# A first weight tile loaded in five uneven parts instead of two even ones, in a DMA-bound sliding-window matmul

One NeuronCore of a Trainium2 chip runs the kernel. The metric is the device time of one launch in microseconds (us). The kernel before takes 182.14 us, median of six runs (181.95 to 182.30).

## The reference

```python
B, S, D, W = 4, 4096, 4096, 64      # x [B,S,D] fp32, w [D,D] fp32
for b in range(B):
    o = int(offsets[b])
    results.append(x[b, o:o+W] @ w)  # four windows of 64 rows, all times the same w
```

All of `w` (67 MB) has to be read once for 256 rows of output.

## The kernel before

The weights are read k tile by k tile (128 rows each) and multiplied in fp16 on the matrix engine (PE). All tiles but the first come over GpSimd's software DMA queue, which converts fp32 to fp16 on the way. The first tile comes as fp32 over the sync queue (SP) and is cast by ScalarE, so that the DMA engines have work before the software queue's first packet, at 5.46 us. A packet is one piece that a DMA engine moves, here a part of one row.

```python
w0_32 = acc[1]                                             # scratch until the sums start
nc.sync.dma_start(out=w0_32[:, :NG], in_=w[0:P, :NG])      # 128 x 2048 fp32, 1 MB
nc.scalar.dma_start(out=off_t[:], in_=offsets[None, :])
nc.sync.dma_start(out=w0_32[:, NG:], in_=w[0:P, NG:])      # the other 1 MB
nc.scalar.copy(out=w_one[0][:, :NG], in_=w0_32[:, :NG])
nc.scalar.copy(out=w_one[0][:, NG:], in_=w0_32[:, NG:])
...
nc.gpsimd.dma_start(out=w_one[1][:], in_=w[P : 2 * P, :])  # software queue: tile 1, x, then the rest
...
q = [nc.scalar, nc.sync]                                   # the last four stores
store(q[g], g, c0, c0 + NG // 2)
```

## Time and profile before

| | before |
|---|---|
| time, median | 182.14 us |
| span in the profile | 180.1 us |
| PE busy | 71% |
| DMA queues, share of 16 engines | 99.7% |
| first weight data; last landing | 1.88; 179.24 us |

The lines of the page, of the windows and of the timeline stand in the prediction below. One more view: the chain of work that ended last, in order of time (start, length, what). Its two long waits for weights before were these:

```profile
6.85 36.17 DMA wc<-in_w_dram
...
78.30 42.09 DMA wc<-in_w_dram
```

The first wide load (4 MB) that the chain waits for is complete at 6.85 + 36.17 = 43.02 us.

Beside these views I use the records of the trace behind them: the start and length of every DMA packet, and the sixteen completion times of every load, one for each DMA engine. A load tells that it has landed by a semaphore, a counter that it raises. "Late" below means behind the median of the sixteen.

### The profile page before, as it was taken

The page shows a single profiled execution, that of the slowest core. Times are in us where ns is not written, and L with a number is a line of the kernel's source. Part 1 is how long each engine was busy: PE and PEld are TensorE (multiplying, and loading weights), DVE is VectorE, ACT ScalarE, POOL GpSimd, SP SyncE. Part 2 cuts the span into 40 slices and gives each one's busy share as a digit, 9 for nine tenths or more (in the row PEclk, how much of TensorE's full clock was granted, in tenths as well). Part 3 has the DMA queues.
Part 4 walks back from the last instruction along what each step waited for, and adds up shares of the span by engine and source line. Part 5 has one row for each costly group of instructions (what it writes and reads, how often), then busy time and mean ns, then how long its engine had stood idle before and what let it go on. Part 6 is the DMA issues. An engine that isn't in the chain of part 4 may idle for free.

```text
span 180.1 us, 1403 instructions
## 1 busy us (share of the span) xinstructions
PE 128.2 (71%) x576; PEld 57.3 (32%) x576; DVE 82.2 (46%) x68; ACT 16.9 (9%) x15; POOL 12.7 (7%) x27
## 2 busy tenths in 40 slices
PE   0000789104999499938996599949999999999910
PEld 0000764001344134413442134414444444443400
DVE  0000566200276427642566036733778975407560
ACT  2422346200000000000000000000000004004000
POOL 4600000000000100010001000020007100000200
PEclk9999999855599969996999569987999999999995
DMA  5999979999998899999989999999999999999996
GB/s 187 313 260 213 286 160 211 236 233 226 233 233 175 182 233 233 236 218 233 204 175 218 233 233 220 222 193 202 229 206 215 198 211 213 214 214 207 338 412 241
DMA packets 4151, 40.97 MB, mean 227 GB/s; under 512 B 434, under 2 KB 434, under 8 KB 2226
## 3 DMA queue, kind: packets, MB, share of 16 engines
q0 software_dynamic: 3280, 36.70, 93.5%
q1 hardware_dynamic: 576, 3.15, 4.6%
q10 hardware_dynamic: 290, 1.05, 1.5%
q8 instruction: 4, 0.07, 0.1%
q14 instruction: 1, 0.01, 0.0%
HBM read 71.30 MB, written 4.19 MB: 419 GB/s over the span
## 4 chain that ended last, share of the span: by engine, by line
DMA 43%; PE 43%; issue 4%; DVE 2%; another core or an unknown queue 1%; POOLq 1%; DVEq 1%; POOL 1%
DMA wc<-in_w_dram 43%; PE banks L154 43%; DVE acc L164 2%; DVEq L263 1%; POOLq L75 1%; POOL xrow L82 0%; POOL identity masks.py:197 0%; POOLq L82 0%; POOL w L71 0%; POOLq masks.py:199 0%; DVEq L164 0%; POOLq L252 0%
## 5 line engine op out<-in xcount | busy, mean ns | idle before, releaser
L154 PE MATMUL banks<-wc,xT 128*128 128x512 f16 x480 | 115.8, 405 | 23.6 <-DMA wc<-in_w_dram 23.3
L164 DVE TENSOR_TENSOR acc<-acc,banks 128x1024 f32<-128x1024 f32 x56 | 67.9, 1221 | 69.0 <-PE banks L154 68.4
L154 PEld LDWEIGHTS <-xT 128*128 128x128 f16 x512 | 52.3, 103 | 93.9 <-DMA wc<-in_w_dram 26.4
L140 PE MATMUL banks<-identity,xrow 128*128 128x128 f16 x64 | 5.3, 261 | 19.9 <-DMA xrow<-in_x_dram 19.9
L209 ACT COPY tmp<-banks 128x1024 f32<-128x1024 f32 x4 | 3.9, 1016 | 128.2 <-PE banks L154 128.2
L149 DVE CAST xT<-banks 128x1024 f16<-128x1024 f32 x4 | 4.8, 1222 | 21.5 <-PE banks L140 21.5
L99 POOL DMA_DIRECT2D wc<-in_w_dram x8 | 4.3, 539 | 108.1 <-PE banks L154 108.1
L140 PEld LDWEIGHTS <-xrow 128*128 128x128 f16 x64 | 5.1, 127 | 20.0 <-issue 20.0
L154 PE MATMUL banks<-w,xT 128*128 128x512 f16 x32 | 7.1, 379 | 0.0
L182 DVE COPY acc<-banks 128x1024 f32<-128x1024 f32 x4 | 4.9, 1225 | 1.6 <-PE banks L154 1.6
L118 POOL DMA_DIRECT2D wc<-in_w_dram x6 | 3.9, 674 | 17.1 <-PE banks L154 17.1
L213 DVE TENSOR_TENSOR acc<-acc,tmp 128x1024 f32<-128x1024 f32 x4 | 4.7, 1218 | 0.0
L151 ACT CAST xT<-banks 128x1024 f16<-128x1024 f32 x4 | 4.0, 1014 | 7.9 <-PE banks L140 7.9
L184 ACT COPY acc<-banks 128x1024 f32<-128x1024 f32 x4 | 4.0, 1012 | 3.0 <-PE banks L154 3.0
L200 POOL DMA_DIRECT2D out_dram<-acc x2 | 1.1, 537 | 27.2 <-DVE acc L213 27.2
L68 ACT CAST w<-acc 128x2048 f16<-128x2048 f32 x1 | 1.9, 1898 | 4.8 <-DMA acc<-in_w_dram 4.8
L82 POOL DMA_DIRECT2D xrow<-in_x_dram x4 | 2.1, 524 | 2.1 <-issue 2.1
L67 ACT CAST w<-acc 128x2048 f16<-128x2048 f32 x1 | 1.9, 1898 | 3.1 <-DMA acc<-in_w_dram 3.1
L67 ACT ACT_TABLE_LOAD x1 | 1.3, 1283 | 1.4 <-PEq L252 1.4
L71 POOL DMA_DIRECT2D w<-in_w_dram x1 | 0.7, 660 | 0.8 <-POOLq L252 0.8
masks.py:199 POOL TENSOR_SCALAR_AFFINE_SELECT identity<-identity 128x128 f16<-128x128 f16 x1 | 0.3, 287 | 0.1
masks.py:197 POOL MEMSET identity<- 128x128 f16 x1 | 0.2, 223 | 0.0
(4 smaller groups left out, 0.4 us busy)
## 6 DMA issues: line engine op xcount, KB each, us to landing
wc<-in_w_dram POOLq DMA_DIRECT2D x5, 4096.0 KB, 42.1
wc<-in_w_dram POOLq DMA_DIRECT2D x4, 1024.0 KB, 24.5
wc<-in_w_dram POOLq DMA_DIRECT2D x1, 3072.0 KB, 37.1
acc<-in_w_dram SPq DMA_DIRECT2D x2, 1024.0 KB, 8.1
xrow<-in_x_dram POOLq DMA_DIRECT2D x4, 512.0 KB, 14.4
wc<-in_w_dram POOLq DMA_DIRECT2D x1, 2048.0 KB, 26.4
out_dram<-acc POOLq DMA_DIRECT2D x2, 1024.0 KB, 5.6
w<-in_w_dram POOLq DMA_DIRECT2D x1, 1024.0 KB, 11.8
```

Of the source, the lines that this page charges most:

```text
L67: nc.scalar.copy(out=w_one[0][:, :NG], in_=w0_32[:, :NG])
L99: nc.gpsimd.dma_start(out=t[:, base : base + r * N], in_=w[k0 * P : (k0 + r) * P, :].rearrange("(p r) n -> p (r n)", r=r),)
L118: nc.gpsimd.dma_start(out=t[:, pos : pos + n * wd].rearrange("p (t n) -> p t n", t=n), in_=w[ki * P : (ki + n) * P, ng * NG + c0 : ng * NG ...
L140: nc.tensor.matmul(out=pairs[t][:, i * P : (i + 1) * P], lhsT=x_cols(g, 8 * t + i), rhs=identity[:], start=True, stop=True,)
L149: nc.vector.tensor_copy(out=dst, in_=pairs[t][:])
L151: nc.scalar.copy(out=dst, in_=pairs[t][:])
L154: nc.tensor.matmul(out=banks(bank), lhsT=xT[g][:, kt * P : (kt + 1) * P], rhs=rhs, start=start, stop=stop,)
L164: nc.vector.tensor_add(out=dst, in0=dst, in1=banks(bank, n))
L182: nc.vector.tensor_copy(out=dst, in_=banks(b0, 2))
L184: nc.scalar.copy(out=dst, in_=banks(b0, 2))
L209: nc.scalar.copy(out=tmp[g][:], in_=banks(4 * g + 2, 2))
L213: nc.vector.tensor_add(out=dst, in0=dst, in1=tmp[g][:])
```

## The change

The intent, as I read it: a load of 12 rows uses twelve DMA engines and one of 4 rows four of them, so the parts 12, 4 and 112 take a row of 4 KB from four engines and give one more to four others. As the first DMAs of the queue the small parts should, by this intent, cost nothing.

```diff
     w0_32 = acc[1]
-    nc.sync.dma_start(out=w0_32[:, :NG], in_=w[0:P, :NG])
+    Q = N // 4
+    for r0, r1, c0, c1 in (
+        (0, 12, 3 * Q, N),
+        (12, 16, 3 * Q, N),
+        (0, P, 0, NG),
+        (16, P, 3 * Q, N),
+        (0, P, NG, 3 * Q),
+    ):
+        nc.sync.dma_start(out=w0_32[r0:r1, c0:c1], in_=w[r0:r1, c0:c1])
     nc.scalar.dma_start(out=off_t[:], in_=offsets[None, :])
-    nc.sync.dma_start(out=w0_32[:, NG:], in_=w[0:P, NG:])
```

## The prediction

> **What bounds the kernel now.** I began with the page: the rows of 40 slices, the queues and the HBM total.
>
> ```profile
> PE   0000789104999499938996599949999999999910
> DMA  5999979999998899999989999999999999999996
> q0 software_dynamic: 3280, 36.70, 93.5%
> q1 hardware_dynamic: 576, 3.15, 4.6%
> q10 hardware_dynamic: 290, 1.05, 1.5%
> q8 instruction: 4, 0.07, 0.1%
> HBM read 71.30 MB, written 4.19 MB: 419 GB/s over the span
> ```
>
> PE has low slices. DMA has one low slice at each edge and is at eight tenths or more elsewhere, apart from one 7. Its queues add up to 99.7% of the sixteen engines' span. So I asked the view of windows where DMA work starts and ends. The last two columns are DMA share and GB/s.
>
> ```profile
> 1.00:1.50 0.50, 0.00 (x0) 0.00 (x0) 0.00 (x0) 0.08 (x1) 0.11 (x1) 1.00 0.00 0
> 1.50:2.00 0.50, 0.00 (x0) 0.00 (x0) 0.00 (x0) 0.50 (x1) 0.50 (x1) 1.00 0.64 131
> 2.00:2.50 0.50, 0.00 (x0) 0.00 (x0) 0.00 (x0) 0.50 (x1) 0.42 (x3) 1.00 0.98 147
> 3.50:4.00 0.50, 0.00 (x0) 0.00 (x0) 0.00 (x0) 0.00 (x0) 0.46 (x1) 1.00 1.00 426
> ...
> 177.50:178.00 0.50, 0.00 (x0) 0.00 (x0) 0.00 (x0) 0.00 (x0) 0.00 (x0) 0.50 1.02 410
> 178.00:178.50 0.50, 0.00 (x0) 0.00 (x0) 0.00 (x0) 0.00 (x0) 0.00 (x0) 0.50 0.54 213
> 178.50:179.00 0.50, 0.00 (x0) 0.00 (x0) 0.00 (x0) 0.00 (x0) 0.00 (x0) 0.50 0.06 25
> ```
>
> (In these lines the figure before the DMA share is the granted clock.) Data moves from about 1.9 to about 178.4 us with hardly a gap, and the stores at the end go straight on after the loads. 71.30 + 4.19 = 75.49 MB in 176.5 us is 428 GB/s, or 26.7 GB/s for each of 16 engines. The kernel is bound by DMA end to end. Only three things can move its end: idle time of the DMA engines, packet overhead, and an uneven share between them. The chain of waits puts 43% on PE, because PE still has queued work after a late load, but the loads and stores behind it have no gap either.
>
> The timeline of the first microseconds shows the part that changes:
>
> ```profile
> 0.87 0.38 SPq L64 DMA_DIRECT2D acc<-in_w_dram  x1
> 1.30 0.42 SPq L66 DMA_DIRECT2D acc<-in_w_dram  x1
> 5.80 1.90 ACT L67 CAST w<-acc 128x2048 f16<-128x2048 f32 x1 [3.10 <-DMA acc<-in_w_dram]
> 12.53 1.90 ACT L68 CAST w<-acc 128x2048 f16<-128x2048 f32 x1 [4.83 <-DMA acc<-in_w_dram]
> 18.31 3.40 PE L140 MATMUL banks<-identity,xrow 128*128 128x128 f16 x32 [18.31 <-DMA xrow<-in_x_dram]
> 25.21 7.07 PE L154 MATMUL banks<-w,xT 128*128 128x512 f16 x32
> ```
>
> SP issues one DMA per 0.43 us (0.87 to 1.30). The first data packet starts at 1.88 us in the packet records, 1.01 us after its issue. The casts of the first k tile end at 14.43, and PE uses them only at 25.21, so 10.8 us are spare: when this tile lands is not on the path. What matters is what its transfer does to the engines.
>
> **Uneven engines.** Every load leaves sixteen completion times, one for each DMA engine. In the last weight load eleven engines finish from 167.7 to 168.3 us and the other five at 168.62, 168.82, 169.01, 169.09 and 169.33. The records also hold five fetches of instructions after the start (four of 16 KB, about 0.9 us each, and one of 8 KB, 0.32 us) at 31.9, 75.5, 111.7, 116.2 and 151.3 us. After each of them one more engine is late in all later loads. So five engines carry something extra, and the latest sets each landing.
>
> **What the Trainium skill says.** "DMA: Bandwidth & Descriptors", section "Why a DMA increments its semaphore by 16 and not by 1", says that a DMA is cut over the largest k up to 16 that divides its slowest dimension, and that from the SP and ACT queues the lowest k engines are used. Twelve rows would then go to engines 0 to 11 and four rows to 0 to 3, one row each, and 112 rows to all, seven each. The trace does not name engines; the [1, 4] load of the offsets leaves one completion packet where a load of 128 rows leaves sixteen, which agrees on k. The same page, "Queues, rings and completion order", says that each engine alternates between its queues; the two queues' packets interleave from 5.5 to 12.5 us here. Thirdly, "Runtime: NRT & Kernel Launch", section "Instruction fetch mechanics", gives 16 KiB blocks, which are the four packets seen; which DMA engines carry them no page that I read says.
>
> **The change, part by part.** The order of instructions differs on SP alone: five loads in place of two, none with a wait. Bytes are unchanged.
> (a) Moved share: engines 0 to 3 get 17 quarter rows of the second half, 4 to 11 get 16 and 12 to 15 get 15. A quarter row is 4096 B; at 26.7 GB/s that is 0.153 us. The intent must be that engines 12 to 15 are the ones with the 16 KB fetches. If so they gain 0.15 us, while 0 to 3 lose 0.15 us out of more than 0.5 us of room. If the late engines are others, this gains nothing or loses 0.15 us.
> (b) Packets: 4096 B packets on the hardware queues took 0.159 us, 8192 B packets 0.309 us. Sixteen of the first less eight of the second: 2.544 - 2.472 = +0.07 us for every engine. Two or three more completion packets of 0.009 to 0.022 us add about 0.03 us. Sum +0.1 us.
> (c) Late start: the first large load is now third on SP. With 0.43 us an issue it begins 2 x 0.43 = 0.86 us later, at about 2.74. In that gap engines move no, one or two quarter rows (0, 0.15, 0.31 us of work). Counted with (a), every engine has the same 15 quarter rows left behind the gap, so all lose 0.86 - 0.15 = 0.71 us against before, with (b) 0.8 us. This is idle time at the front of a saturated stream, and nothing later gives it back.
> (d) Against (c): the start is slow already. Eight packets at 0.309 us from 1.88 would end at 4.35, but the first load's completions come from 4.84 to 5.43, mean 5.13; counted from each engine's own first packet some 0.6 us is lost. First packets took 0.37 to 1.1 us in place of 0.31, while 131 and 147 GB/s moved. If that is a cold start which the small loads now pay inside the gap, up to 0.6 us comes back; if each load after an idle gap pays it anew, none does.
> I take two thirds of (d), 0.4 us: 0.71 + 0.1 - 0.4 = +0.4 us. A shorter distance from issue to data for the second and third loads than the 1.01 us of the first would take off up to another 0.4; half of that leaves +0.2 us.
>
> **Rivals.** First, the rebalancing works as meant: the start's idle time is hidden by the cold start and the late engines save a row, giving -0.15 us or a little more, 182.0. For it: 12, 4 and 112 are exactly the numbers that take a row from engines 12 to 15. Against: SP's issue rate. Second, the full delay: nothing of the cold start is absorbed, +0.8 us, 182.95. For it: no DMA slack anywhere. Third, a PE effect: after a wait PE ran at half the clock (427 ns a matmul against 216 from 120.5 to 123.8); a load landing late against the clock's steps could lengthen a slow stage, at most one step of 3.4 us, 1.7 us of work. Stores now wait for DMA rather than for PE (the last store's add ends at 174.2, its data start at 176.9, about 1.7 us of slack after 1.0 us of issue), which hides most of this: under +0.7 us. Fourth, a later first tile stalls the casts: excluded by the 10.8 us.
>
> **Range and chances.** Runs before lay within 0.16 us. The cases span 182.0 to 183.0, so I predict 182.35 us, with 181.85 to 182.95 for 8 in 10. Two per cent is 3.6 us, which no case reaches.
>
> **What would show it.** SP should issue at about 0.87, 1.30, 1.73, 2.16 and 2.59. If (c) holds, the DMA share between 2.0 and 3.0 us falls well below 0.88, the mean of before's two windows, and the sixteen landings of all later loads shift late together. If the first rival holds, the late engines' landings come 0.15 us earlier and those of four on-time engines later. The prediction is wrong if the casts or PE's last stage set the end, or if the late engines are among 0 to 3, which would add 0.15 us.

## The result, and the profile after

The changed kernel takes 183.76 us, median of six (183.69 to 184.54), against 182.14: 1.62 us more. The ratio is 1.0101, interval 1.0081 to 1.0121; ratios here are the mean time of one kernel's fast runs over that of the other's in the same rounds, so not quite the ratio of the medians. It is a loss clear of noise, and 0.8 us above the top of my range (182.95).

Four rows of the page of after:

```profile
PE   0000769302999499947997499949999999999900
DMA  5999999999799999998999999988999899999995
q1 hardware_dynamic: 736, 3.15, 4.8%
HBM read 71.30 MB, written 4.19 MB: 416 GB/s over the span
```

The bytes are the same, the hardware queue has 736 packets in place of 576, and the rate fell from 419 to 416 GB/s. DMA still bounds the kernel end to end. The windows at both edges (the last two columns are DMA share and GB/s; a packet counts where it starts), first two of before that the prediction doesn't show, then those of after:

```profile
2.50:3.00 0.50, 0.00 (x0) 0.00 (x0) 0.00 (x0) 0.20 (x1) 0.13 (x1) 1.00 0.78 262
3.00:3.50 0.50, 0.00 (x0) 0.00 (x0) 0.00 (x0) 0.00 (x0) 0.00 (x0) 1.00 0.81 311
```

```profile
2.00:2.50 0.50, 0.00 (x0) 0.00 (x0) 0.00 (x0) 0.50 (x1) 0.42 (x3) 1.00 0.13 33
2.50:3.00 0.50, 0.00 (x0) 0.00 (x0) 0.00 (x0) 0.20 (x1) 0.13 (x1) 1.00 1.57 262
3.00:3.50 0.50, 0.00 (x0) 0.00 (x0) 0.00 (x0) 0.00 (x0) 0.00 (x0) 1.00 0.32 115
...
178.50:179.00 0.50, 0.00 (x0) 0.00 (x0) 0.00 (x0) 0.00 (x0) 0.00 (x0) 0.50 1.04 418
179.00:179.50 0.50, 0.00 (x0) 0.00 (x0) 0.00 (x0) 0.00 (x0) 0.00 (x0) 0.50 0.94 377
```

From 2.0 to 2.5 us only 33 GB/s move where 147 moved before. Then sixteen first packets start together (share 1.57) and are slow (115 GB/s in the next half microsecond, where before had 311). The stores run about one microsecond longer. The timeline of after:

```profile
0.87 2.09 SPq L72 DMA_DIRECT2D acc<-in_w_dram  x5
10.10 1.90 ACT L74 CAST w<-acc 128x2048 f16<-128x2048 f32 x1 [7.40 <-DMA acc<-in_w_dram]
21.86 1.90 ACT L75 CAST w<-acc 128x2048 f16<-128x2048 f32 x1 [9.86 <-DMA acc<-in_w_dram]
26.27 7.07 PE L161 MATMUL banks<-w,xT 128*128 128x512 f16 x32
```

SP issued five loads in 2.09 us, 0.42 each, as foreseen. The second half of the tile was complete only at 21.76 us in place of 12.51: each 4 KB packet waited its turn behind a packet of the software queue (0.64 us on average), so fifteen of them per engine lasted longer than eight of 8 KB. The cast and the first multiplication moved by 9.3 and 1.1 us. The chain of after has the same two waits:

```profile
6.84 37.56 DMA wc<-in_w_dram
...
79.61 42.08 DMA wc<-in_w_dram
```

The first wide load is complete at 44.40 in place of 43.02 us, 1.38 later; the second wait is as long as before (42.08 to 42.09). So the transfers lost their time before 44 us, and nothing of it later. The latest engine carries other delays too (an instruction fetch, in the prediction's reading), so for the sums I take the mean of the sixteen completions of this load: 42.05 before, 43.26 after, **+1.21 us**. The last landing of the kernel moved from 179.24 to 180.34, +1.10.

But the span grew by 1.49. The rest is at the very end. Before it is over, SP waits for the semaphore of every DMA in turn. The view of SP's waits, before and after (total us, times, longest):

```profile
SPq L263 <- DMA out_dram<-acc: 4.2, 4, 1.9
```

```profile
SPq L270 <- DMA out_dram<-acc: 4.4, 2, 3.2
```

Before, the four last stores were met one after the other, and the last store's semaphore was last in SP's list: 0.91 us from the last landing (179.24) to the end of the span. After, ten hardware DMAs share eight semaphores, the last store uses that of the first small load again, and this stands early in the list. When it came at 180.36, six more waits of 0.06 us each and what follows them were still to be gone through: 1.29 us from the last landing to the end, **+0.38 us**.

A last part lies outside the profiled span. In the recorded runs the time exceeds the span by 2.00 us on average in after (six runs) and by 1.84 in before (28 runs); of the kernels below on the same chip as before's first rounds, five_big_first has 1.99 and the others 1.82 to 1.87. So the difference of the medians is about the span's 1.49 and this 0.16; what the 0.16 is, no run shows.

### The profile page after: what moved, and what is told of

Read it like the earlier page. It is cut to its first block, busy times and chain, and to the rows that moved or that the text cites. A ratio compares the mean times of both kernels' runs of the same rounds, so it can differ in the third digit from the quotient of the medians.

```text
span 181.6 us, 1414 instructions
## 1 busy us (share of the span) xinstructions
PE 128.1 (71%) x576; PEld 57.3 (32%) x576; DVE 82.2 (45%) x68; ACT 16.6 (9%) x15; POOL 12.7 (7%) x27
## 4 chain that ended last, share of the span: by engine, by line
DMA 44%; PE 42%; issue 4%; DVE 2%; another core or an unknown queue 1%; POOLq 1%; DVEq 1%; POOL 1%
DMA wc<-in_w_dram 44%; PE banks L161 42%; DVE acc L171 2%; DVEq L270 1%; POOLq L82 1%; POOL xrow L89 0%; POOL identity masks.py:197 0%; POOLq L89 0%; POOL w L78 0%; POOLq masks.py:199 0%; DVEq L171 0%; POOLq L259 0%
```

## The experiments

My theory after this reading is a sum: a late start, the 4 KB packets, and the end. The rival is that the uneven share itself made an engine late. Fourteen kernels ran; all gave correct results. Medians are of four runs, all in the fast state (the two marked kernels ran once, state unknown), beside before on the same chip (182.05 to 182.11). `dummy` is a scratch tile that a run adds. The diffs are against before (five_big_first: against after) and are shortened. "Mean" is again the mean completion of the first wide load, 42.05 us in the profile of before.

### 1. The small parts last: five_big_first

```diff
-        (0, 12, 3 * Q, N), (12, 16, 3 * Q, N), (0, P, 0, NG), (16, P, 3 * Q, N), (0, P, NG, 3 * Q),
+        (0, P, 0, NG), (0, P, NG, 3 * Q), (16, P, 3 * Q, N), (0, 12, 3 * Q, N), (12, 16, 3 * Q, N),
```

> The same five loads of the changed kernel on SP, but with the two small ones last. My theory is a sum: the DMA engines idle some 0.75 us while SP issues the two small loads first, the two hardware-generated loads of 4 KB packets and their mixing with the software queue cost 0.1 to 0.5 us, and the waits at the very end cost 0.37 us because ten hardware DMAs share semaphores where before seven did not. This order takes away the idle start alone, so 182.4 to 182.9 us, with the first weight data at 1.9 us as before. Rival: the uneven share (one quarter row more for four engines, one less for four others) is itself the loss; then it stays at 183.6 to 183.9 us.

Measured: 183.39 us, in two pairs, 182.99 and 183.13, 183.66 and 183.68; ratio 1.0076. Mean 42.68, from the last landing to the end 1.29. The late start is gone, and 0.57 of the 1.21 us of mean with it. The median is above what I expected; the lower pair is near, and the upper pair lies where the rival had it. That pair doesn't speak for the rival, though I can't explain it: single runs 0.6 to 0.9 us above the others occur in after (184.4 and 184.5), in two_tiny_first (183.83) and in before itself (182.86 beside 182.05).

### 2. The late start alone: two_tiny_first

```diff
+    for i in range(2):
+        nc.sync.dma_start(out=dummy[0:1, 4*i : 4*i+4], in_=w[0:1, 4*i : 4*i+4])   # 16 bytes each
     nc.sync.dma_start(out=w0_32[:, :NG], in_=w[0:P, :NG])
```

> The kernel before, with two loads of 16 bytes into a scratch tile ahead of the large loads on SP, so the start is late but no share of an engine changes. My theory: the first large load starts 0.8 us later, nothing gives it back, and the end has a semaphore used twice too: 183.1 to 183.5 us. Rival (uneven share): 182.1 to 182.3 us. Rival (a cold start that only has to be paid once, by whoever comes first): 182.3 to 182.7 us.

Measured: 183.00 us, ratio 1.0062, a little under my range. Mean 42.65, +0.60; 1.36 us from the last landing to the end. Its windows at the start:

```profile
2.00:2.50 0.50, 0.00 (x0) 0.00 (x0) 0.00 (x0) 0.50 (x1) 0.42 (x3) 1.00 0.00 0
2.50:3.00 0.50, 0.00 (x0) 0.00 (x0) 0.00 (x0) 0.20 (x1) 0.13 (x1) 1.00 1.40 262
3.00:3.50 0.50, 0.00 (x0) 0.00 (x0) 0.00 (x0) 0.00 (x0) 0.00 (x0) 1.00 0.51 180
```

No data moves for half a microsecond, and the start after it is slow again. Delay alone, without a byte moved to another engine, makes +0.60 us of transfer. The rival of the uneven share foresaw no loss; it can't be the whole. The rival of a cold start that is paid once foresaw 182.3 to 182.7 us. As 0.45 us of the time is the end's, the time alone doesn't exclude it, and the tiny loads are one packet each, so most engines had moved nothing before. The trace of after is the better witness, under (d) below.

### 3. The packets alone: even_split

```diff
-    nc.sync.dma_start(out=w0_32[:, NG:], in_=w[0:P, NG:])
+    nc.sync.dma_start(out=w0_32[:, NG : NG + NG // 2], in_=w[0:P, NG : NG + NG // 2])
+    nc.sync.dma_start(out=w0_32[:, NG + NG // 2 :], in_=w[0:P, NG + NG // 2 :])
```

> The kernel before, with the second half of the first tile loaded as two loads of all 128 rows by 1024 columns: packets of 4 KB, even shares, no late start, eight hardware DMAs in all so that no semaphore is used twice. It prices the packets alone. My theory: 182.2 to 182.6 us, and the first tile's second half lands at 17 to 21 us in place of 12.5, since packets of two queues alternate one for one. Rival (packet size and mixing are the main loss): 183.0 us or more.

Measured: 182.61 us (182.59 to 182.73), ratio 1.0030, with an interval of 0.9999 to 1.0061 since before scattered in these rounds. Mean 42.71, +0.66; the end is as before (0.93 us). The chain shows it:

```profile
6.86 37.00 DMA wc<-in_w_dram
...
79.01 42.14 DMA wc<-in_w_dram
```

The second half's sixteen 4 KB packets took 2.99 us per engine (0.187 each), where eight of 8 KB took 2.57 (0.321 each): +0.42. The software queue's packets beside them took 0.13 more. The first packets started 0.16 later, but the first half's packets then took 0.12 less. The price of a 4 KB packet isn't a fixed one: those of the first of the two loads took 0.202 us, those of the second, which alternated with software packets too, 0.171. At 0.171 sixteen would cost only 0.17 more than before; why the first load was slower isn't shown. Late start and packets, 0.60 + 0.66 = 1.26, meet the 1.21 of the whole change.

### 4. The end alone: three_tiny_last

```diff
     nc.sync.dma_start(out=w0_32[:, NG:], in_=w[0:P, NG:])
+    for i in range(3):
+        nc.sync.dma_start(out=dummy[0:1, 4*i : 4*i+4], in_=w[0:1, 4*i : 4*i+4])
```

> The kernel before, with three loads of 16 bytes on SP behind the large ones: nothing late, nothing moved, ten hardware DMAs in all like the changed kernel. It prices the end alone. My theory: the span from the last landing to the end grows from 0.9 to 1.3 us and the time to 182.4 to 182.6 us. If the end is not charged for semaphores used twice: 182.1 to 182.2 us.

Measured: 182.43 us (182.37 to 182.44); ratio 1.0017 with an interval (0.9986 to 1.0048) that one run of before at 182.86 widens. Mean 42.09, unmoved; the end 1.29 in place of 0.91. SP's waits are those of after in kind, two in place of four, the longest for the last store:

```profile
SPq L266 <- DMA out_dram<-acc: 4.7, 2, 3.4
```

Ten hardware DMAs in place of seven cost the end 0.38 us.

### 5. One more DMA, or smaller packets: rows_split, rows_stride, quarters_woven, first_half_split, one_load

```diff
 # rows_split: second half as rows 0-63 and 64-127; rows_stride: as every other row
+    for r0, r1 in ((0, P // 2), (P // 2, P)):
+        nc.sync.dma_start(out=w0_32[r0:r1, NG:], in_=w[r0:r1, NG:])
+    for r in range(2):
+        nc.sync.dma_start(out=w0_32[r:P:2, NG:], in_=w[r:P:2, NG:])
```

> The second half of the first tile as two loads of 64 rows by 2048 columns: one more DMA than before, as in even_split, but packets stay 8 KB. If the packets of 4 KB cost the 0.56 us that even_split lost, this is at 182.0 to 182.3 us and the first wide load lands at 42.1 us on average, as before; if one more DMA costs it, 182.5 to 182.7 us and 42.7 us.

> The second half as two loads of every other row, 8 KB packets. Against rows_split, whose loads each went to one half of the partitions and lost 1.9 us, each load here is spread over all partitions. If the half of the partitions was what cost there, 182.0 to 182.7 us here, where 182.0 to 182.2 means that one more DMA is free and 182.5 to 182.7 that it is what even_split paid for; if any load of 64 rows costs it, 183.5 us or more.

rows_split took 183.97 us, ratio 1.0098, mean 43.25: a surprise that fits neither theory. Its packets in the second half took 0.36 to 0.64 us on average from one microsecond to the next, in place of 0.32. Each of its loads goes to one half of the partitions only (partitions are the 128 rows of a tile). rows_stride, with as many DMAs and rows in each but spread over all partitions, took 182.25 us, ratio 1.0015, mean 42.09, with packets of 0.32. The first wide wait in the chain, first rows_split, then rows_stride:

```profile
6.84 37.39 DMA wc<-in_w_dram
6.87 36.12 DMA wc<-in_w_dram
```

So one more DMA with 8 KB packets is nearly free, and loads to one block of 64 partitions are not; why their packets are slower isn't shown.

```diff
 # quarters_woven: two loads, each of two separate quarters of the columns (4 KB pieces everywhere)
+    halves = lambda a: a.rearrange("p (h t n) -> p h t n", h=2, t=2)
+    nc.sync.dma_start(out=halves(w0_32[:])[:, :, 0, :], in_=halves(w[0:P, :])[:, :, 0, :])
+    nc.sync.dma_start(out=halves(w0_32[:])[:, :, 1, :], in_=halves(w[0:P, :])[:, :, 1, :])
 # first_half_split: the first half as two loads of 1024 columns, the second half as before
 # one_load: nc.sync.dma_start(out=w0_32[:], in_=w[0:P, :]), nothing else
```

> Two loads as before, but the first takes the first and third quarter of the columns and the second the second and fourth: all 512 packets of the first tile are 4 KB, with no DMA more and no share changed. If each packet of 4 KB costs more than half of one of 8 KB (even_split and first_half_split lost 0.55 us with half of the tile in such packets), this is 0.7 to 1.2 us slower than before, 182.8 to 183.3 us. If the third DMA cost it: 182.0 to 182.3 us.

> The first half of the tile as two loads of 1024 columns (4 KB packets) and the second half in one of 8 KB packets. The first half moves before the software queue has begun, so 4 KB packets run alone. If the cost of 4 KB packets comes from alternating with the software queue's packets, 182.1 to 182.3 us; if it comes from the packets wherever they run, or from the start, 182.5 us or more.

> The whole first tile as one load of 128 rows by 4096 columns, packets of 16 KB, one DMA less. If smaller packets cost time by their number, this should gain: 181.5 to 181.9 us. If only packets under 8 KB cost anything: 182.0 to 182.2 us. The first cast then waits for the whole tile, some 11 us, and has room.

quarters_woven took 184.42 us, ratio 1.0146, mean 43.85: the direction foreseen, twice the size. Its 4 KB packets took 0.214 us each, SP needed 0.63 us to issue each load and the first data came at 2.29 us, so part of it is a late start once more. It has the number of DMAs of before, so one more DMA is not needed for the loss: its packets took 1.22 us more per engine than those of before, and the start was 0.41 us later. first_half_split took 182.65 us, ratio 1.0033 with an interval (0.9994 to 1.0072) that holds 1, mean 42.42 (+0.37; its 4 KB packets took 0.17 us more per engine than the first half of before). That points to a cost of 4 KB packets also before the software queue runs, but is too small to be called shown. one_load took 182.46 us, ratio 1.0017 with an interval that holds 1, mean 42.27: my hope that still larger packets gain is a miss.

### 6. Which engines fetch instructions: mark_twelve, mark_four

```diff
     nc.sync.dma_start(out=w0_32[:, NG:], in_=w[0:P, NG:])
+    for i in range(2):
+        for c in (0, NG):
+            nc.sync.dma_start(out=acc[0][0:12, c : c + NG], in_=w[0:12, c : c + NG])   # mark_four: 0:4
```

> The kernel before with four more loads of 12 rows by 8 KB on SP, into a buffer that is overwritten later. They put four 8 KB packets, 1.24 us, on twelve of the sixteen engines (0 to 11, if the page on DMA holds), so these twelve are late from then on and four are not. Time 183.0 to 183.9 us. If the four engines with the 16 KB instruction fetches are the other four, as the change seems to suppose, the last weight load shows four engines about 0.6 us behind the earliest possible, eleven at about 1.2 and one at about 1.5; if the fetches are among the twelve, one to four early engines at 0 and some late ones at about 1.8 to 2.1 us.

> As mark_twelve, with loads of 4 rows: four engines, 0 to 3 if the page holds, become late by at least 1.2 us. In mark_twelve two of the 16 KB fetches fell on the four engines that it left alone, and two did not. Here the last weight load shows whether any of the other two falls on the marked four: such an engine would stand about 1.0 us behind its three companions. If none does, five engines out of the early twelve are late, as before.

The times, 187.25 and 185.49 us in one run each, are above what I expected: the packets of the small loads took 0.58 and 0.54 us each in place of 0.31. The marks worked. How far each engine's completion lies behind the second one, in three loads of mark_twelve (own reading of the records; 16 KB fetches at 39.1, 79.9, 118.5 and 156.9 us, one of 8 KB at 113.3):

```
first completion at 24.45: 0.0 0.0 0.1  0.2  | 3.0 3.1 3.1 3.1 3.1 3.2 3.3 3.6 3.7 3.7 3.7 3.8
first completion at 44.03: -.1 0.0 0.1  1.3  | 1.8 1.9 1.9 2.0 2.1 2.2 2.3 2.5 2.6 2.7 2.9 3.0
first completion at 170.1: -.1 0.0 0.95 1.2  | 1.8 1.9 1.9 2.1 2.4 2.4 2.5 2.7 2.8 2.9 3.2 3.3
```

Twelve engines are marked and four are not. The first two 16 KB fetches fall on two of the four unmarked engines and make them about 1.0 to 1.3 us late; the other two unmarked ones stay on time to the end, so the later fetches fall among the twelve. In mark_four all four 16 KB fetches fall on the twelve unmarked engines (in the last load 0.84, 1.02, 1.07 and 1.44 us late), and after the 8 KB fetch one of the marked four is 0.4 us later. The Trainium skill ("DMA: Bandwidth & Descriptors", "Why a DMA increments its semaphore by 16 and not by 1") says that such loads use the lowest-numbered engines; no run here shows it, for the trace doesn't number them. Read with it, and if the fetches fall on the same engines in both runs: two of the four 16 KB fetches lie on 12 to 15, two on 4 to 11, and the 8 KB fetch on 0 to 3. The share of the change would then relieve two of four late engines and leave the latest where it was.

### 7. The share alone, doubled: share_8k

```diff
-    nc.sync.dma_start(out=w0_32[:, NG:], in_=w[0:P, NG:])
+    for r0, r1 in ((0, 12), (12, 16), (16, P)):
+        nc.sync.dma_start(out=w0_32[r0:r1, NG:], in_=w[r0:r1, NG:])
```

> The uneven share alone, without the late start and without 4 KB packets: first half first, then the second half as loads of 12, 4 and 112 rows of 8 KB, twice the shift of the changed kernel (0.31 us off engines 12 to 15, 0.31 us onto 0 to 3). Nine hardware DMAs, so the end costs up to 0.4 us. By the marks two of the four engines with 16 KB fetches are among 12 to 15 and two are not, so the latest engine of the last weight load stays about 1.1 us behind the median and the share gains nothing: 182.3 to 182.7 us. If the share gains where it is not spoiled: under 182.2 us, with the late engines at most 0.8 us behind. If loads of 112 rows, which fall across the partitions otherwise than those of 128, are slow in themselves: 182.9 us or more.

Measured: 184.02 us, ratio 1.0094, far above the 182.3 to 182.7 that I expected; mean 42.82, the latest engine 1.37 us late in the last weight load, 1.35 us at the end. Shifting twice as much, from the middle of the queue, is worse than not shifting: packets of the hardware queue took 0.43 to 0.52 us on average from 5 to 8 us, when the loads of 12 and 4 rows ran. The share gains nothing here, and blocks of few partitions cost, as in rows_split. With the small 4 KB parts last this cost is not to be seen: five_big_first (with the share) and even_split (without) have means of 42.68 and 42.71, and their latest engines are 1.09 and 1.12 us late in the last weight load. The changed kernel itself isn't clear of it: the software queue's first 384 packets took 0.41 us per engine more than in before, as in share_8k (0.44), where even_split and five_big_first have 0.13 and 0.12. A mean can't show the share as such, for what some engines lose others gain; that takes the latest engine. It is 1.10 us late in after and 1.18 in before, and 1.06 in three_tiny_last, which shifts nothing: a gain of 0.1 us can't be told from the scatter.

### 8. Attempts to beat both: two_queues, scalar_second

```diff
 # two_queues                                            # scalar_second keeps the offsets first on scalar
-    nc.scalar.dma_start(out=off_t[:], in_=offsets[None, :])
-    nc.sync.dma_start(out=w0_32[:, NG:], in_=w[0:P, NG:])
+    nc.scalar.dma_start(out=w0_32[:, NG:], in_=w[0:P, NG:])
+    nc.sync.dma_start(out=off_t[:], in_=offsets[None, :])
```

> An attempt to beat both: the second half goes out on the scalar queue at the same time as the first half on the sync queue, and the offsets follow on sync, where they have room. Each DMA engine then has two queues to draw from in the slow first microsecond. If the cold start is a latency that a second queue hides, up to 0.4 us are gained: 181.7 to 181.9 us. If it is a rate limit of the memory, 182.0 to 182.2 us.

> two_queues lost 2.5 us because the offsets stood behind a megabyte on the sync ring and landed at 11 us, so the DMA engines ran dry from 12 to 14 us. Here the offsets stay first on the scalar queue and the second half follows behind them there, 0.5 us after the first half on sync. If two queues hide part of the cold start: 181.7 to 181.9 us. If not: 182.0 to 182.3 us.

two_queues took 184.53 us, ratio 1.0146. Its windows show why:

```profile
12.00:13.00 1.00, 0.00 (x0) 0.00 (x0) 0.00 (x0) 1.00 (x2) 0.53 (x1) 1.00 0.49 98
13.00:14.00 1.00, 0.00 (x0) 0.00 (x0) 0.00 (x0) 1.00 (x2) 0.53 (x1) 1.00 0.86 115
```

The offsets, 32 bytes, stood behind the first half in SP's ring and landed at 11.07 us in place of 2.04. The windows of `x` were issued only at 12.31, and the DMA engines ran short for two microseconds. scalar_second, with that mended, took 182.08 us (182.00 to 182.18), ratio 0.9990, interval 0.9961 to 1.0018: the same as before. A second queue doesn't hide the slow first microsecond: with both halves on the way from the start, two_queues moved 98, 180 and 213 GB/s in the three half microseconds from 2.0 us, where before moved 147, 262 and 311. No version that I tried beats the kernel before.

### The sum

| part | shown by | us |
|---|---|---|
| late start of the large loads | two_tiny_first, mean | +0.60 |
| 4 KB packets in the second half | even_split, mean | +0.66 |
| the small loads, put last | five_big_first against even_split, mean | -0.03 |
| end: semaphores used twice | three_tiny_last | +0.38 |
| sum | | +1.61 |
| measured, medians | | +1.62 |

The parts were measured apart, each in one profile; that they add up this closely is luck. The span itself grew by 1.49, of which the last landing has 1.10 and not 1.21, and 0.16 of the medians' difference lies outside the span. By the medians of four runs the parts come to 0.95 (two_tiny_first, end included) + 0.56 (even_split) = 1.51. So I take the parts as right to some 0.15 us.

## Why the prediction was wrong

The steps that failed are terms of its sum: it had +0.11 us for the start after what the cold start and a shorter way were to give back (0.71 - 0.4 - 0.2), +0.1 for the packets and nothing for the end. The runs showed +0.60, +0.66 and +0.38.

**The bound** was right: transfers fill the engines from the first packet to the last, and what the start loses reaches the end.

**(a) The share.** The skill's rule for the number of engines held (twelve marked, four not). What I called the intent fails because the fetches are not all on the four relieved engines: two of the four 16 KB fetches fell on others (mark_twelve). The prediction had allowed for this. The share alone moved nothing that could be told from scatter.

**(b) Packets and (d) cold start: here the sum failed.** I priced a 4 KB packet at the 0.159 us of undisturbed ones, for +0.1 us in all. In the mix they took 0.187, and the neighbours slowed: +0.66. This term was mis-sized by more than half a microsecond; the 0.66 is the whole loss of even_split, and why its packets slowed stays open. And I let the cold start give back 0.4 us of the delay, on the thought that the small loads would pay it in the gap. They didn't: the slow start came again after them. In after, the eight packets per engine of the first half took 3.05 us, 0.58 over 8 x 0.309, as much as the excess of before (5.64 less 8 x 0.309 and 8 x 0.322 is 0.59). It was paid anew. The further 0.2 us for a shorter way from issue to data was 0.07 (third issue near 1.71, first large packet at 2.65: 0.94 against 1.01).

**(c) The late start** was right in kind and about right in size. The large load's first packets started at 2.78 us on average in place of 2.02, 0.76 later (I had 0.86), and two_tiny_first shows 0.60 us of it in the mean completion (I had 0.71 after the row moved in the gap). The sign that I had named for it was a poor one: the DMA share from 2.0 to 3.0 us was 0.85 against 0.88, since slow packets count as busy; the rate fell from 205 to 148 GB/s. The other sign came true: all later loads land about 1.2 us late in the mean.

**What I left out.** The end's waits, +0.38 us. I counted the added loads' completion packets and not that they make the last store share a semaphore.

**The rivals.** The first (a gain of 0.15) fell. The second (the full delay, 182.95) was the nearest: its 0.7 us of delay met 0.60, but it held neither of the other terms. The third, PE's clock, played no part: PE's stage from the wide load at 120.4 us to the end had the same half-clock step of 3.4 us, from 120.4 before and from 121.6 after, and the last landing followed the transfers. The fourth was rightly excluded for the end, though the second cast moved by 9.3 us and used up nearly all of the 10.8 us that I had called spare.

**What stays open:** why single runs of after, five_big_first, two_tiny_first and before lie 0.6 to 0.9 us above the others; what the 0.16 us outside the span is; why packets of 4 KB, and packets to blocks of few partitions, slow each other and the software queue; and how these two share the loss in the changed kernel itself.

## What to carry to other kernels

In a kernel whose DMA engines never idle, a late start is not given back (0.60 of 0.76 us here): issue the largest, widest load first, and put small ones behind it, unless something waits for them as the windows of `x` wait for the offsets. Before shifting rows between DMA engines, find out with a marked load which engines are late; and check what the shift does to packet size and to the spread over partitions, for each cost more here than the imbalance was worth. Count the DMAs of a queue up to the end: a store that reuses an early semaphore makes the last wait of the kernel longer.

## What the Trainium skill lacked or had wrong

- "DMA: Bandwidth & Descriptors", "Specifications", has 512 B as the least transfer for line rate. Undisturbed, pieces of 4 KB took 0.159 us and pieces of 8 KB 0.309, which agrees; on the hardware queue mixed with software DMAs sixteen of 4 KB took 2.99 us per engine where eight of 8 KB took 2.57 (even_split). The page doesn't tell the two cases apart.
- The same page, "Rules for kernel authors", says of two transfers to disjoint partition halves that they serialize and that one transfer of 128 partitions is to be used. The advice agrees, but serializing isn't the whole reason here: with blocks of 64 partitions the kernel lost 1.9 us, with every other partition, two loads on one queue as well, 0.2 us (rows_split, rows_stride).
- No page that I read says which DMA engines carry instruction fetches. Here a 16 KB fetch makes its engine about 1 us late for the rest of the kernel, and four fetches fell on four different engines (mark_twelve, mark_four).
- No page that I read has the slow start of the first load after idle: first packets of 8 KB took 0.37 to 1.1 us in place of 0.31, some 0.6 us per engine in all (before), and in after, where twelve engines moved a quarter row first and a gap followed, 0.51 to 1.01 us and 0.58 in all once more.
- No page that I read has the cost of the waits at a kernel's end: 0.06 us for each semaphore that stands behind the last one to come, 0.38 us in all here (three_tiny_last).
